# Wider norm sums, dilated attention cut into steps, six banks for two tails, and held condition sums in a four-layer block stack

## The chip, the core and the metric

The kernel runs on one core of one Trainium2 chip. The metric is the device time of one execution in microseconds (us). In the texts PE is TensorE (matrix products; its clock is granted at one of two levels, 2.4 or 1.2 GHz), PEld its weight loads, DVE is VectorE, ACT is ScalarE, POOL is GpSimd and SP is SyncE, which issues the transfers from memory.

## The reference, cut to what matters

Four residual layers stand one behind the other, each on 256 tokens of 1024 values. The first two (the first block) end each half with a layer norm; the second two (the second block) begin each part with an rms norm. The parts that the change touches:

```python
def layer_norm(x, g, b):
    xf = x.astype(jnp.float32)
    xc = xf - jnp.mean(xf, -1, keepdims=True)
    var = jnp.mean(xc * xc, -1, keepdims=True)
    return (xc * lax.rsqrt(var + LN_EPS) * g.astype(jnp.float32) + b.astype(jnp.float32)).astype(x.dtype)
...
    # first block, layer i: mixer (retention, then neighbourhood attention), feed-forward
        m_lat = jnp.split(cond_lat @ ada_w[i] + ada_b[i], 6, axis=-1)
        h_lat = layer_norm(DEEPNORM_ALPHA * h_lat + m_lat[2] * y_lat, ln_g[i, 0], ln_b[i, 0])
        f_lat = swiglu(modulate(h_lat, m_lat[3], m_lat[4]), ffn_w13[i], ffn_w2[i])
        h_lat = layer_norm(DEEPNORM_ALPHA * h_lat + m_lat[5] * f_lat, ln_g[i, 1], ln_b[i, 1])
...
    # second block, layer l: feed-forward, hybrid mixer, feed-forward
        u = modulate_2(rmsnorm(h, ln_mix[l]), sh2, sc2)
        m = hybrid_mixer(u, w_in[l], conv_w[l], a_log[l], dt_bias[l], dn_norm[l], w_a[l], w_b[l], w_o[l])
        h = h + gt2[:, None, :] * m
...
    # in hybrid_mixer: a gated delta rule of 8 heads, and dilated attention of 12 heads of 64
    for window, dilation in DA_PATTERNS:
        o_p, lse_p = dilated_window_branch(qd, kd, vd, slopes, window, dilation)
    ...
    y_b = o_b.reshape(B, S, DA_WIDTH) @ w_b
    merged = jax.nn.sigmoid(gate_a) * y_a + jax.nn.sigmoid(gate_b) * y_b
    return merged @ w_o
```

Layer 0 carries a second stream of 256 tokens (the context) through both halves.

## The kernel before

All tokens lie along the columns: h is [128, 8, 256], eight blocks of 128 features by 256 tokens. Every weight product is made three times (high by high, high by low, low by high), with both operands split into a high part fp32r and the rest. Weights are streamed: SP loads a chunk of 128x1024 into w_raw, ACT makes w_hi, DVE makes w_lo, a few chunks ahead of use. One product row is 256 or 512 tokens wide and takes its weights from the chunk.

The order of all instructions is written by the program itself and kept on the chip (a manual schedule): each engine executes its own instructions in the order in which they are emitted. While the products are emitted, other work (generators called sides) is pumped in between. class Times (line 29) keeps planned times: busy is a clock for each engine, when() gives the time at which a tile is planned to be written or read. A side yields WAIT when its next step isn't due by PE's planned clock; with force set it emits regardless.

- Norm (line 692): squares by ACT, then sums over the features by PE. sums (line 767) takes the tile as stationary operand and a tile ones [128, 1] as the moving one, so that each sum is one column. In fp32 one such product is two records in the trace. stats (line 782) reads the sums, makes mean and scale, and spread copies them over 128 rows by four transposes (ident,n_st).
- PSUM has eight banks: four acc, two mm, two tr. bank(many) (line 304) takes a bank of mm, or with many=True the earlier of mm and acc. outp(3), the last retention output products (line 1269), and the last part of Layer0's feed-forward (line 1381 on) run with many=False, so on the two mm banks.
- ada_gen (line 434) makes the condition vectors on DVE: the products of a weight tile are added into ada_acc, a transpose and a reduction make ada_part, and reduce_one (line 486) folds it by one PE product into a tr bank.
- The hybrid (class at line 1660, its run at 1697): projections into q, k, v of the delta rule, z, and the dilated q, k, v; the chains of the delta rule and the convolutions are sides. dilated (line 2093) treats six pairs of heads ("a head" below is one n, its two 64-row halves i = 0 and 1). first makes the scores of both halves in two tr banks, adds the distances (DVE), takes two maxima per half (DVE) and two exponentials per half (ACT). normalize multiplies and sums (DVE), and scales (ACT). second(0) and second(1) transpose (PE) and copy (ACT) one half each; third multiplies with the values (PE) and splits the result (ACT ah, DVE al). pipeline (line 255) emits the stage that is due, the last stage first.
- gate_b: the products of the second gate come in four pairs; their evacuation writes into sb, where the dilated values lie, so the second pair first calls finish on the dilated side:

```python
        def gate_b(i):
            if i:
                da.finish()
            p = (i + 3) % 4
            return sb[:, 2 * p:2 * p + 2, :]
...
    def finish(self):
        while not self.done:
            self.b.forced(self.step)
```

## Time and profile before

| | |
|---|---|
| median of 3 runs | 2873.59 us (2870.81 to 2875.27) |
| profiled execution | 2875.96 us |
| its span | 2874.1 us |
| mean granted clock of PE | 0.977 |
| busy: PE, PEld | 2776.9 us (97%), 2548.0 us (89%) |
| busy: DVE, ACT, POOL | 2097.7 us (73%), 1322.0 us (46%), 290.0 us (10%) |

The profiled execution's time is its span and 1.9 us around it. Busy time of PE counts an instruction until its modelled end, so PE's rows overlap; the distance of two starts is what one costs. The granted clock is a share of 2.4 GHz: 0.50 is 1.2 GHz. A stretch of the trace is read by the engines' busy times in it and its granted clock; the timeline gives each row's start, its length and, in brackets, the idle time ahead of it with the instruction that ended it.

### The profile page before, as it was taken

The numbers are of one execution on the slowest core, as the hardware profiler recorded it, in microseconds if no ns is written. First come the engines' busy times: TensorE is split into PE (matmuls) and PEld (weight loads), VectorE is DVE, ScalarE is ACT, GpSimd is POOL, SyncE is SP. The second block draws the span as 40 slices with busy tenths as digits, with TensorE's granted clock in tenths as the row PEclk, the third lists the DMA queues.
The fourth block names the chain that finished last, engine by engine and source line by source line (L and its number), as shares of the span: only waits on it lengthen the run. The fifth ranks groups of instructions, "written<-read, shape, count | busy, mean of one in ns | idle before, by whom it ended". The sixth has DMA issues, their size and how long they took to land.

```text
span 2874.1 us, 49237 instructions
## 1 busy us (share of the span) xinstructions
PE 2776.9 (97%) x19349; PEld 2548.0 (89%) x19349; DVE 2097.7 (73%) x3396; ACT 1322.0 (46%) x2318; POOL 290.0 (10%) x363
## 2 busy tenths in 40 slices
PE   8999998999998998998999989999999999999999
PEld 4878887888877778998999989999999998899999
DVE  5888886887877776787877777788565577676754
ACT  4433323422224544444445665554454456655543
POOL 0000002000002100001002123210010022130100
PEclk9999998999998998998999999999999999999999
DMA  7444441576755543775886533458566654324564
GB/s 232 155 129 144 141 154 63 190 234 211 239 180 144 122 149 117 253 255 157 267 261 199 155 92 115 147 173 273 186 181 184 186 172 118 89 82 153 179 183 133
DMA packets 433245, 488.34 MB, mean 170 GB/s; under 512 B 34651, under 2 KB 362301, under 8 KB 433013
## 3 DMA queue, kind: packets, MB, share of 16 engines
q1 hardware_dynamic: 431972, 484.59, 54.1%
q8 instruction: 152, 2.49, 0.4%
q10 hardware_dynamic: 1040, 0.60, 0.1%
q14 instruction: 81, 0.66, 0.1%
HBM read 484.07 MB, written 1.05 MB: 169 GB/s over the span
## 4 chain that ended last, share of the span: by engine, by line
PE 82%; DVE 8%; ACT 4%; issue 3%; DMA 1%; SPq 1%; POOL 1%; ACTq 0%; DVEq 0%; POOLq 0%
PE ps_acc L75 46%; PE ps_mm L75 32%; PE ps_tr L75 4%; DVE w_lo L75 2%; ACT w_hi L75 2%; DVE n_t L75 1%; DMA ada_w<-ada_w 1%; ACT n_a L75 1%; DVE n_a L75 1%; DVE h L75 1%; DVE al L75 1%; SPq L75 1%; DVE ada_acc L75 0%; DVE da_st L75 0%; ACT ah L75 0%
## 5 line engine op out<-in xcount | busy, mean ns | idle before, releaser
L75 DVE TENSOR_TENSOR w_lo<-w_raw,w_hi 128x1024 fp32r<-128x1024 f32 (+1 forms) x672 | 816.5, 1226 | 426.5 <-ACT w_hi L75 420.8
L75 ACT ACTIVATE w_hi<-w_raw 128x1024 fp32r<-128x1024 f32 (+2 forms) x686 | 699.7, 1032 | 490.3 <-PE ps_acc L75 233.9
L75 PE MATMUL ps_mm<-ah,w_hi 128*128 128x256 f32 (+1 forms) x2288 | 707.0, 309 | 8.1 <-DVE q_lo L75 3.0
L75 PE MATMUL ps_mm<-ah,w_lo 128*128 128x256 f32 (+1 forms) x2288 | 680.8, 298 | 4.0 <-POOL w_lo L75 2.3
L75 PE MATMUL ps_mm<-al,w_hi 128*128 128x256 f32 (+1 forms) x2288 | 681.7, 298 | 0.2
L75 PEld LDWEIGHTS ps_mm<-ah,w_hi 128*128 128x128 f32 x2288 | 434.9, 190 | 31.4 <-issue 11.1
L75 PEld LDWEIGHTS ps_mm<-ah,w_lo 128*128 128x128 f32 x2288 | 435.2, 190 | 18.9 <-POOL w_lo L75 3.4
L75 PEld LDWEIGHTS ps_mm<-al,w_hi 128*128 128x128 f32 x2288 | 435.7, 190 | 12.4 <-DVE al L75 1.0
L75 PE MATMUL ps_acc<-ah,w_hi 128*128 128x256 f32 (+2 forms) x1440 | 436.4, 303 | 2.3 <-ACT w_hi L75 2.3
L75 PE MATMUL ps_acc<-ah,w_lo 128*128 128x256 f32 (+2 forms) x1440 | 433.5, 301 | 1.4 <-DVE w_lo L75 1.3
L75 PE MATMUL ps_acc<-al,w_hi 128*128 128x256 f32 (+2 forms) x1440 | 433.3, 301 | 0.0
L75 DVE SCALAR_TENSOR_TENSOR ada_acc<-ada_w,cact,ada_acc 128x512 f32<-128x512 f32 x476 | 354.4, 759 | 16.8 <-DMA ada_w<-ada_w 11.8
L75 PEld LDWEIGHTS ps_acc<-ah,w_lo 128*128 128x128 f32 x1440 | 274.7, 191 | 12.5 <-DVE w_lo L75 2.6
L75 PEld LDWEIGHTS ps_acc<-ah,w_hi 128*128 128x128 f32 x1440 | 274.5, 191 | 12.2 <-ACT w_hi L75 2.5
L75 PEld LDWEIGHTS ps_acc<-al,w_hi 128*128 128x128 f32 x1440 | 274.8, 191 | 9.6
L75 PE MATMUL ps_acc<-hh,w_hi 128*128 128x256 f32 (+1 forms) x866 | 255.5, 295 | 0.0
L75 PE MATMUL ps_acc<-hh,w_lo 128*128 128x256 f32 (+1 forms) x866 | 255.2, 295 | 0.0
L75 PE MATMUL ps_acc<-hl,w_hi 128*128 128x256 f32 (+1 forms) x866 | 254.9, 294 | 0.0
L75 POOL TENSOR_TENSOR n_a<-n_a 128x512 f32<-128x512 f32 (+1 forms) x28 | 40.4, 1444 | 1292.6 <-ACT n_a L75 1292.1
L75 PEld LDWEIGHTS ps_acc<-hh,w_hi 128*128 128x128 f32 x866 | 163.2, 188 | 4.4
L75 PEld LDWEIGHTS ps_acc<-hl,w_hi 128*128 128x128 f32 x866 | 163.2, 188 | 4.4
L75 PEld LDWEIGHTS ps_acc<-hh,w_lo 128*128 128x128 f32 x866 | 163.0, 188 | 4.4
(391 smaller groups left out, 4368.5 us busy)
## 6 DMA issues: line engine op xcount, KB each, us to landing
ada_w<-ada_w SPq DMA_DIRECT2D x448, 256.0 KB
w_raw<-w_in SPq DMA_DIRECT2D x132, 512.0 KB
w_raw<-ffn_w SPq DMA_DIRECT2D x128, 512.0 KB
w_raw<-ffn_wg SPq DMA_DIRECT2D x88, 512.0 KB
w_raw<-ffn_wu SPq DMA_DIRECT2D x88, 512.0 KB
w_raw<-ffn_wd SPq DMA_DIRECT2D x80, 512.0 KB
w_raw<-ret_w_in SPq DMA_DIRECT2D x48, 512.0 KB
w_raw<-na_w_qkv SPq DMA_DIRECT2D x24, 512.0 KB
```

Of the source, the lines that this page charges most:

```text
L75: r = f(*args, **kw)
```

## The change

Five edits:

1. The sums use avg (128x128, each value 1/256) as the moving operand in place of ones; each sum becomes 128 equal columns, of which stats reads the first and multiplies by 256/D.
2. outp(3) and the last down part run with many=True.
3. The dilated attention has eight stages in place of five: first, soft(0), soft(1), normalize(0), normalize(1), second(0), second(1), third. The first five have a spare of 1.0: they are due only when DVE's planned busy time is at most 1.0 us ahead of PE's planned clock. The limits name the same stages by their new numbers.
4. In ada_gen a fold waits until the part is planned to be written.
5. warm(16): sixteen products of two constant tiles into an mm bank, between the last layer norm of the first block and the first rms norm.

```diff
-        self.ones = cp.tile([128, 1], F32, name="ones")
-        nc.vector.memset(self.ones, 1.0)
...
-                            if not self.force and self.free("ps_tr", self.BANKS["tr"]) > self.clock:
+                            when = max(self.free("ps_tr", self.BANKS["tr"]),
+                                       self.times.when(self.times.written, self.pending[0][2]))
+                            if not self.force and when > self.clock:
                                 yield WAIT
...
+    def warm(self, n):
+
+        ps = self.ps("mm")
+        for _ in range(n):
+            self.nc.tensor.matmul(ps[:, :128], self.ident, self.avg, start=True, stop=True)
...
-                    nc.tensor.matmul(self.p[i][:, o:o + 1], x[:, 128 * t:128 * t + 128], b.ones,
+                    nc.tensor.matmul(self.p[i][:, 128 * o:128 * o + 128], x[:, 128 * t:128 * t + 128], b.avg,
...
-        p, st = self.p[i], self.s[i][1]["st"]
+        p, st = self.p[i].rearrange("p (a n) -> p a n", n=128)[:, :, 0], self.s[i][1]["st"]
...
-            ts(st[:, 0:4], p[:, 0:4], 1.0 / D, None, op0=OP.mult)
+            ts(st[:, 0:4], p[:, 0:4], 256.0 / D, None, op0=OP.mult)
...
-            return b.gemm_b(self.o[h], lambda k: (yh[:, k, :], yl[:, k, :]), 512, self.residual(gates, norms), ks=4, many=norms is None)
+            return b.gemm_b(self.o[h], lambda k: (yh[:, k, :], yl[:, k, :]), 512, self.residual(gates, norms), ks=4, many=True)
...
-                           self.residual(gates, self.norms if part == NP - 1 else None), ks=2 * (f1 - f0), many=part < NP - 1))
+                           self.residual(gates, self.norms if part == NP - 1 else None), ks=2 * (f1 - f0), many=True))
...
-                st = P.tile([128, 2, 4], F32, name="da_st", bufs=4)
+                S[n].append((s, P.tile([128, 2, 4], F32, name="da_st", bufs=4)))
+
+        def soft(i):
+            def f(n):
+                s, st = S[n][i]
                 for t, (a, z) in enumerate(segs):
                     nc.vector.tensor_reduce(st[:, t, 0:1], s[:, a:z], axis=AX.X, op=OP.max, negate=True)
                 for t, (a, z) in enumerate(segs):
                     nc.scalar.activation(s[:, a:z], s[:, a:z], AF.Exp, bias=st[:, t, 0:1])
-                S[n].append((s, st))
-
-        def normalize(n):
-            for s, st in S[n]:
+            return f
+
+        def normalize(i):
+            def f(n):
+                s, st = S[n][i]
...
-        stages = ((first, lambda: "tr2", (3, lambda: 2)), (normalize, None, None), (second(0), tr, (4, lambda: 1)), (second(1), tr, None),
-                  (third, tr, None))
+        stages = ((first, lambda: "tr2", (6, lambda: 2), 1.0), (soft(0), None, None, 1.0), (soft(1), None, None, 1.0),
+                  (normalize(0), None, None, 1.0), (normalize(1), None, None, 1.0), (second(0), tr, (7, lambda: 1)),
+                  (second(1), tr, None), (third, tr, None))
...
         n.finish()
+        b.warm(16)
         n2 = Norm(b, "rms", slow=False)
```

How the order of the instructions moves, at three places. First PE in Layer1's norm, between the neighbourhood attention's output products (o_hi, o_lo with w_hi, w_lo): before,

```order
L75 MATMUL ps_acc<-o_hi,w_lo 128x256
L75 MATMUL ps_tr<-ones,n_a 128x1 x2
L75 MATMUL ps_tr<-ones,h 128x1 x2
L75 MATMUL ps_tr<-ones,n_a 128x1 x2
L75 MATMUL ps_tr<-ones,h 128x1 x2
```

and after:

```order
L75 MATMUL ps_acc<-o_hi,w_lo 128x256
L75 MATMUL ps_tr<-avg,n_a 128x128 x2
L75 MATMUL ps_tr<-avg,h 128x128 x2
L75 MATMUL ps_tr<-avg,n_a 128x128 x2
L75 MATMUL ps_tr<-avg,h 128x128 x2
```

Nothing moves there; the sums have 128 columns instead of one.

Second, DVE in the first hybrid at the second and the first dilated head (n_a<-da_dist is a score row, da_st<-n_a its maxima, da_mult the normalization; d_ tiles belong to the chains, n_t and cv_x to the convolutions, ada_ to the condition vectors): before,

```order
L75 TENSOR_TENSOR w_lo<-w_raw,w_hi 128x1024
L75 SCALAR_TENSOR_TENSOR n_a<-da_dist,ps_tr 128x384
L75 TENSOR_REDUCE da_st<-n_a 128x1 x2
L75 SCALAR_TENSOR_TENSOR n_a<-da_dist,ps_tr 128x384
L75 TENSOR_REDUCE da_st<-n_a 128x1 x2
L75 SCALAR_TENSOR_TENSOR n_a,da_st<-n_a,da_mult 128x128
L75 SCALAR_TENSOR_TENSOR n_a,da_st<-n_a,da_mult 128x256
L75 RECIPROCAL da_st<-da_st 128x2
```

and after:

```order
L75 TENSOR_TENSOR d_XX<-d_XX,ps_acc 128x256
L75 SCALAR_TENSOR_TENSOR ada_acc<-ada_w,cact,ada_acc 128x512
L75 SCALAR_TENSOR_TENSOR n_a<-da_dist,ps_tr 128x384 x2
L75 TENSOR_TENSOR w_lo<-w_raw,w_hi 128x1024
L75 SCALAR_TENSOR_TENSOR n_t<-cv_x,cwT,n_t 128x255
L75 SCALAR_TENSOR_TENSOR n_t<-cv_x,cwT,n_t 128x254
L75 SCALAR_TENSOR_TENSOR n_t<-cv_x,cwT,n_t 128x253
```

The maxima and the normalization no longer follow the scores; weight splits, convolutions and condition rows come between, and the first head begins later.

Third, PE in the first hybrid at the products of gate_b (ps_mm<-ah or al with w_hi or w_lo; ident,n_a are the transposes of second, da_k,da_q the scores of first, n_t,sb and da_pt,sb the products of third): before, at one of the last two heads of the dilated attention, among the products,

```order
L75 MATMUL ps_mm<-ah,w_lo 128x256
L75 MATMUL ps_acc<-ident,d_XX 128x128 x2
L75 MATMUL ps_acc<-d_XX,d_t_15494 128x128 x2
L75 MATMUL ps_tr<-ident,n_a 128x128 x3
L75 MATMUL ps_mm<-ah,w_hi 128x256
```

and after, behind the last product of the second gate_b pair:

```order
L75 MATMUL ps_mm<-ah,w_lo 128x256
L75 MATMUL ps_tr<-ident,n_a 128x128 x6
L75 MATMUL ps_tr<-da_k,da_q 128x128 x2
L75 MATMUL ps_tr<-da_k,da_q 128x256 x2
L75 MATMUL ps_tr<-n_t,sb 64x128
L75 MATMUL ps_tr<-da_pt,sb 64x128
```

After these rows 27 more of the same four kinds follow before the next weight product: four times the six transposes in all, two times the scores, four times the six products of third, with nothing else on PE between. The second hybrid has a piece of the same form behind its second gate_b pair.

## Rows read from the trace of the kernel before

**Rows 1.** The page: its first line, and the chain by engine.

```profile
span 2874.1 us, 49237 instructions
...
PE 82%; DVE 8%; ACT 4%; issue 3%; DMA 1%; SPq 1%; POOL 1%; ACTq 0%; DVEq 0%; POOLq 0%
```

**Rows 2.** Stretches by engine (columns in the first line), the two norms of the first block.

```profile
core 0: us, PE busy (x) PEld busy (x) DVE busy (x) ACT busy (x) POOL busy (x), PEclk, DMA share, GB/s
1094.00:1097.70 3.70, 2.47 (x21) 2.24 (x20) 2.40 (x5) 2.64 (x7) 0.00 (x0) 1.00 0.40 134
1097.80:1114.80 17.00, 17.00 (x81) 17.00 (x81) 9.18 (x16) 5.15 (x9) 0.00 (x0) 0.50 0.20 63
1316.20:1336.70 20.50, 14.18 (x64) 13.52 (x64) 11.76 (x27) 10.85 (x24) 0.70 (x1) 0.50 0.18 58
```

**Rows 3.** Timeline of PE (start, length, instruction, count): Layer1's norm.

```profile
1098.78 0.99 PE L75 MATMUL ps_tr<-ones,h 128*128 128x1 f32 x4
...
1115.37 0.58 PE L75 MATMUL ps_tr<-ones,n_a 128*128 128x1 f32 x4
...
1119.23 0.60 PE L75 MATMUL ps_tr<-ident,n_st 128*128 128x128 f32 x4
```

**Rows 4.** Timeline of DVE, same stretch; the brackets hold the idle time before, and its end.

```profile
1105.99 0.88 DVE L75 SCALAR_TENSOR_TENSOR h<-ps_acc,v_lat,h 128x256 f32<-128x256 f32 x2 [1.95 <-PE ps_acc L75]
...
1116.44 0.16 DVE L75 TENSOR_SCALAR n_st<-ps_tr 128x4 f32<-128x4 f32 x1 [5.18 <-PE ps_tr L75]
```

**Rows 5.** Timeline of PE: Layer0's first norm, the first block's last norm, the end.

```profile
471.76 0.47 PE L75 MATMUL ps_mm<-v_hi,w_hi 128*128 128x512 f32 x1 [3.66 <-DVE h L75]
...
486.65 1.12 PE L75 MATMUL ps_tr<-ident,n_st 128*128 128x128 f32 x4 [1.43 <-POOL n_st L75]
...
1325.52 1.87 PE L75 MATMUL ps_tr<-ones,n_a 128*128 128x1 f32 x8 [3.95 <-ACT n_a L75]
...
2865.37 4.02 PE L2232 MATMUL ps_acc<-ident,h 128*128 128x128 f32 x16 [0.51 <-DVE h L2226]
```

**Rows 6.** Timeline of PE, first hybrid: the longest wait.

```profile
1675.81 1.22 PE L75 MATMUL ps_acc<-d_XX,d_t 128*128 128x128 f32 x4 [4.84 <-DVE d_MQ L75]
```

**Rows 7.** Stretches by engine: the half-clock piece, and 80 us of each hybrid.

```profile
1674.60:1681.40 6.80, 5.59 (x26) 5.59 (x27) 4.73 (x18) 3.55 (x9) 0.73 (x1) 0.50 0.45 126
1660.00:1740.00 80.00, 71.52 (x587) 66.71 (x587) 57.36 (x153) 48.80 (x126) 14.19 (x22) 0.96 0.32 96
2428.00:2508.00 80.00, 71.42 (x589) 66.57 (x588) 53.83 (x146) 49.44 (x129) 14.76 (x23) 0.96 0.27 80
```

**Rows 8.** Timeline of DVE: half a head (scores, maxima), then normalization of two halves.

```profile
1711.37 0.56 DVE L75 SCALAR_TENSOR_TENSOR n_a<-da_dist,ps_tr 128x384 f32<-128x384 f32 x1
...
1713.59 0.28 DVE L75 SCALAR_TENSOR_TENSOR n_a<-n_a,da_mult 128x128 f32<-128x128 f32 x1
...
1714.35 0.64 DVE L75 SCALAR_TENSOR_TENSOR n_a<-n_a,da_mult 128x128 f32<-128x128 f32 x1
```

**Rows 9.** Timeline of ACT: exponentials or scalings of two halves, copies, a gate.

```profile
1671.28 1.54 ACT L75 ACTIVATE n_a<-n_a,da_st 128x128 f32<-128x128 f32 x4 [0.82 <-DVE da_st L75]
...
1697.34 0.49 ACT L75 ACTIVATE n_t<-ps_tr 128x384 f32<-128x384 f32 x1
...
1737.52 0.39 ACT L75 ACTIVATE ah<-ps_tr 128x256 fp32r<-128x256 f32 x1 [0.43 <-PE ps_tr L75]
...
1767.27 0.60 ACT L75 ACTIVATE sb<-ps_mm 128x512 f32<-128x512 f32 x1
```

**Rows 10.** Timeline of PE: scores of one head, transposes, first and last product with values.

```profile
1664.76 1.29 PE L75 MATMUL ps_tr<-da_k,da_q 64*128 64x128 f32 x8
...
1695.89 0.32 PE L75 MATMUL ps_tr<-n_t,sb 128*64 128x128 f32 x1
...
1696.50 0.27 PE L75 MATMUL ps_tr<-da_pt,sb 128*64 128x128 f32 x1
...
1700.06 0.49 PE L75 MATMUL ps_tr<-ident,n_a 128*128 128x128 f32 x3
```

More of the change, by code (lines that the diff above doesn't have):

```diff
@@ L791, in stats @@
         else:
-            ts(st[:, 0:2], p[:, 0:2], 1.0 / D, EPS, op0=OP.mult, op1=OP.add)
+            ts(st[:, 0:2], p[:, 0:2], 256.0 / D, EPS, op0=OP.mult, op1=OP.add)
         nc.gpsimd.tensor_tensor(out=st[:, 0:2], in0=st[:, 0:2], in1=b.mhalf[:, 0:2], op=OP.pow)
@@ L2129, in normalize @@
                     nc.scalar.activation(s[:, a:z], s[:, a:z], AF.Copy, scale=st[:, t, 2:3])
+            return f
         def second(i):
```

## The prediction

> **What bounds the kernel now.** I read the page's chain first: TensorE (PE) holds 82% of it, VectorE (DVE) 8%, ScalarE (ACT) 4% [rows 1]. So a microsecond counts only where PE stands still or runs at 1.2 GHz instead of 2.4. I then asked for stretches with their granted clock, and for PE's timeline where the stretch was slow. Two kinds of places came out that the change touches. The first kind is the norms. In Layer1's norm PE was busy 17.00 of 17.00 us, and yet the granted clock was 0.50, the 1.2 GHz level [rows 2]. What PE did before the fall was one-column sums, back to back. The same sums take 0.99 us for four records at the half clock and 0.58 at the full one, and four 128-column transposes take 0.60 at the full one, as much as four one-column records [rows 3]. So PE's time is the same for 1 and for 128 columns; what can differ is the clock that is granted after them. The second kind is the hybrids. There PE waits 4.84 us for DVE's d_MQ [rows 6], since DVE first does two heads' scores and a whole normalization; the half clock of the next 6.8 us follows from that wait [rows 7].
>
> **The sums with 128 columns, and the warm matmuls.** They remove and add no PE time by themselves; the gain is the clock. I take each place by what ends last there.
> - Layer1's norm: at the full clock 17.0 us of PE work would be 8.5, the most there is. DVE waits 1.95 and 5.18 us for PE in it, 7.1 together [rows 4]; beyond that DVE and ACT bound. The last spread at 1119.23 [rows 3] would come near 1113. I take 6, from 4.5 to 7.1.
> - Layer0's first norm, with the six banks for the last retention products: PE waits 3.66 us for DVE's h, because the two mm banks are full. Six banks let PE go on, but DVE still has the same h to add, so a part only moves. With it the tail speeds up: eight sums by 0.41 (0.99 less 0.58) per four records at the half clock, the four transposes of the spread from 1.12 to 0.60 [rows 3, 5]. I take 3, from 0 to 5.5. Layer0's second norm has the same form with its last part down: 2.5, from 0 to 5.5.
> - The first block's last norm: 20.5 us at the half clock, PE busy 14.18 [rows 2]. Half of that, 7.1, is the ceiling, but in its middle PE waits for ACT's n_a, 3.95 us first [rows 5]. Only the ends count: I take 3, from 1 to 5. The 16 warm matmuls are 32 records; eight take 1.87 us at the half clock [rows 5], so they need about 7 us there and 3.5 at the full one. At the full clock they fit in the 3.95 us wait and cost nothing; at the half clock 3 us would stick out. That end is in the range.
> - The end: sixteen transposes take 4.02 us [rows 5], and at the full clock about 2; ACT's copies behind them take part of that. I take 1.5, from 0 to 2.
> Sum of the norms: 16, from 6 to 25.
>
> The Trainium skill, page "TensorE: Matmul & The Clock Gate", Part 1, "What's actually happening", says that the gate follows how busy PE has been recently. Rows 2 speak against it as it stands: PE was busy all the time and had 1.2 GHz. By that rule the wider sums would bring nothing, and of the 16 only the banks' part would stay.
>
> **The condition sums held.** The fold of a finished condition sum waits until DVE is planned to have written it. Up to the second norm the order of the instructions is unchanged but for the shapes and banks, so the waits there stay. Later it moves a fold of a quarter us here and there. I take 0, from -2 to 2.
>
> **The dilated attention in steps: what it removes.** In 80 us of each hybrid PE is busy 71.52 and 71.42, so it stands still 8.5 and 8.6 us; and in the 6.8 us at half clock half of 5.59 us of work is lost, 2.8 in the first and by the same form about 2.4 in the second [rows 7]. Together 22. The new order has half as much of DVE's dilated work in one piece: two scores, then a weight split, and the maxima rows later (the order of DVE above). But with these gaps DVE gets convolution and condition rows; a wait of 1 to 2 us remains in places. I take 19, from 10 to 22. What is late next is the step that waits for ACT's copy of a chain, some tenths each.
>
> **What it adds.** The five first stages start only when DVE's planned backlog is at most 1 us. They are so put off that when the second gate_b pair's evacuation calls da.finish(), more than three of six heads are still open. finish() forces them, and PE's order shows it: 24 transposes, two heads' scores and four products with values stand in one piece with no weight product between (the order of PE above). Before, the last head's copy was at 1737.52 and this evacuation at 1767.27, so nothing was forced [rows 9]. PE executes in order, so the later products wait, though their weights are there. The same happens in both hybrids.
>
> Price, first hybrid. ACT has 13 pairs of exponentials or scalings at 0.77 (1.54 for two), 8 copies at 0.49 and 4 at 0.39 [rows 9]: 15.5 us. DVE has 6 pairs of maxima, two heads' scores, 7 normalizations and 4 subtractions: scores with maxima are 1.11 per half (1711.37 to 1713.59 for two), a normalization 0.76 [rows 8], a subtraction about ACT's 0.39: 12.4. PE has 8 transposes of three, two scores and four products with values, from 0.88 (1695.89 to 1696.77), 1.29 and 0.49 [rows 10], less the overlap of neighbours: 7.5. If ACT alone bound, the piece lasts 15.5; if nothing overlaps, 35. Followed through the order row by row (a score needs both ps_tr banks, so it waits for the copies of the head before; a product with values needs both halves' copies; each row begins when its engine and what it reads are free), it comes to 23. PE's 7.5 stood among products before, so PE loses 15.5, from 8 to 27. The second hybrid has 11 pairs, 6 copies and 4 heads' ends: ACT 13, all 31; followed through, 22, of which PE works 7: loss 15, from 6 to 24.
>
> To this comes the clock. One wait of 4.84 us brought 6.8 us at 1.2 GHz, most of it after PE had work again [rows 6, 7]. A piece in which PE works a third of the time will run mostly at 1.2: I add 3 us inside each and 2.5 after each, 11 together, from 0 to 13. Added in both: 15.5 + 15 + 11 = 41, from 14 to 64; I believe 32 to 46.
>
> **The sum.** 2875.96 (the profiled execution) - 16 (norms) - 19 (waits removed) + 41 (forced pieces) = 2882. The runs' median, 2873.59, lies 2.4 under the profiled one, so I say 2880, 6 us or 0.2% slower. About 0.2% is what a measurement of this kernel can tell from no change.
>
> **Rivals.**
> 1. The forced pieces are nearly hidden: DVE and ACT come to them with a lead, PE enters late, and the clock holds. The mechanism is in gate_b(1): if the open heads' maxima and scalings are done before PE gets there, only ACT's bound is left, 8 + 6 = 14 for both. Then 2874 - 16 - 19 + 14 = 2853. It decides from the point where the pieces together cost less than 35 (16 + 19); from 29 down it is faster by over 0.2%. For it: ACT is busy only some 60% of these 80 us [rows 7]. Against it: the last weight product and the first forced row have nothing but a few chain rows between them.
> 2. The wide sums don't hold the clock (the rule of the skill's page, worked out by rows): of the norms' 16 only the banks' 3 stay, so 2880 + 13 = 2893. For it: PE was fully busy and the clock fell all the same; what it counts, these rows don't say. Against it: the 128-column transposes at 1119.23 run at 0.60 for four, the full clock [rows 3], and the hybrids are full of such rows at a granted clock of 0.96 in the mean [rows 7].
> 3. The steps don't remove the waits: condition rows on DVE take the place of the dilated ones, so the 22 us stay with new names. Removed 5 rather than 19: 2894. For it: the new order has condition rows among the steps in the first hybrid (the order of DVE above). Against it: the second hybrid has none left.
> 4. The change doesn't do what it says, in the norms' timeline: the three or four places at half clock are off the chain, gain under 6 and the pieces as said: 2890. It is counted with rival 2.
>
> **Chances.** Forecast 0.50 (slower 0.30, within 0.2% 0.20, since it lies at that edge); rival 1 0.25 (faster 0.22, same 0.03); rival 2 with 4 0.13 (slower 0.11, same 0.02); rival 3 0.12 (slower 0.08, same 0.04). So faster 0.22, same 0.29, slower 0.49. The forecast's own range is 2868 to 2890. The range of 8 in 10 leaves out the best of rival 1 and the worst of 2 and 3: 2855 to 2898.
>
> **What would show it.** Right: in both hybrids, just before the second tanh of sb, PE's timeline shows waits for ACT's n_a, n_t and da_pt of 10 to 18 us in sum over 20 to 27 us, at 0.50 over part of it; and the 4.84 us wait for d_MQ is gone. In Layer1's norm the granted clock is 1.00 and its 17 us are about 11. Wrong: waits there under 7 us in each hybrid (rival 1), 0.50 in Layer1's norm (rival 2), or idle time above 6 us per hybrid ahead of the forced piece (rival 3).

## The result, and the profile after

The changed kernel takes 2888.34 us (median of 4 runs, 2887.55 to 2890.55), the kernel before 2874.24 beside it: a ratio of 1.0052, 95% interval 1.0035 to 1.007. It is slower by 14 us, where 6 us were forecast; the time lies in the range. The profiled execution took 2890.55 us.

The page after, its first lines and the chain [rows 1]:

```profile
span 2888.8 us, 49302 instructions
## 1 busy us (share of the span) xinstructions
PE 2775.7 (96%) x19381; PEld 2534.4 (88%) x19381; DVE 2097.6 (73%) x3395; ACT 1324.0 (46%) x2318; POOL 293.3 (10%) x363
...
PE 77%; DVE 11%; ACT 6%; issue 3%; DMA 2%; POOL 0%; SPq 0%; ACTq 0%; DVEq 0%; POOLq 0%
```

Laid beside each other at the same instructions, the two traces say where the 14 us come from. At the first norm's spread the changed kernel is 2.0 us ahead; at Layer0's second norm 5.2 more; at Layer1's norm 6.8 more; from there, over the first block's last norm, to the start of the first hybrid 4.5 more, 18.5 us in all. The first hybrid then loses 19.4 us and the second 15.7; the feed-forwards behind them and the end give back 2.0. Sum: -18.5 + 35.1 - 2.0 = 14.6 us, but for rounding the difference of the spans (2888.8 to 2874.1). The first of these numbers is good to some us only: the traces of kernels of this study whose instructions are the same up to the first hybrid reach it between 1508.4 and 1514.9 us.

Stretches of the changed kernel, by engine, with the granted clock: Layer1's norm (two rows), the half-clock pieces in the first and second hybrid, and the 196 us ahead of each of these pieces.

```profile
core 0: us, PE busy (x) PEld busy (x) DVE busy (x) ACT busy (x) POOL busy (x), PEclk, DMA share, GB/s
1084.00:1100.00 16.00, 13.59 (x96) 12.82 (x96) 11.61 (x24) 7.88 (x15) 0.00 (x0) 0.89 0.27 83
1100.00:1109.00 9.00, 9.00 (x79) 9.00 (x78) 4.24 (x9) 1.64 (x4) 0.70 (x1) 1.00 0.19 58
1767.80:1791.70 23.90, 19.53 (x92) 12.99 (x93) 9.87 (x40) 12.46 (x32) 0.74 (x1) 0.50 0.00 0
2535.80:2556.30 20.50, 14.38 (x64) 8.72 (x65) 8.19 (x40) 11.47 (x31) 0.00 (x0) 0.50 0.00 1
1566.00:1762.00 196.00, 180.41 (x1474) 172.67 (x1475) 149.02 (x327) 118.66 (x315) 58.74 (x82) 0.98 0.41 122
2333.00:2529.00 196.00, 186.57 (x1538) 180.51 (x1538) 139.44 (x300) 119.25 (x296) 50.30 (x76) 0.98 0.39 117
```

In Layer1's norm the 17 us at 0.50 [rows 2] are gone: the clock is 0.89 and then 1.00. In the hybrids two new stretches of 23.9 and 20.5 us stand at 0.50. There PE executes the forced piece. Its timeline in the first hybrid, cut to the longest waits, the scores and the end:

```profile
1762.07 0.49 PE L75 MATMUL ps_tr<-ident,n_a 128*128 128x128 f32 x3
1765.17 0.84 PE L75 MATMUL ps_tr<-ident,n_a 128*128 128x128 f32 x3 [2.60 <-ACT n_a L75]
1766.63 0.48 PE L75 MATMUL ps_tr<-da_k,da_q 64*128 64x128 f32 x2 [0.63 <-ACT n_t L75]
1767.70 1.60 PE L75 MATMUL ps_tr<-da_k,da_q 64*128 64x128 f32 x6 [0.58 <-ACT da_pt L75]
...
1773.38 2.35 PE L75 MATMUL ps_tr<-da_k,da_q 64*128 64x128 f32 x8
...
1780.46 1.09 PE L75 MATMUL ps_tr<-ident,n_a 128*128 128x128 f32 x3 [1.75 <-ACT n_a L75]
...
1789.01 1.22 PE L75 MATMUL ps_acc<-d_XX,d_MT 128*128 128x128 f32 x4
```

From 1762.07 to 1789.01 there is no weight product. The waits in brackets are those that the prediction named, for ACT's n_a, n_t and da_pt and shortly for DVE. Together they come to 8.1 us here and 7.6 in the second hybrid. The clock falls behind the first three of them, at 1767.8, and stays at 0.50 until 1791.7, just after the weight products are back; most of the rest of the loss is the clock's, by an estimate below.

Ahead of the piece the waits were to vanish. The waits of the changed kernel's PE from 1566 to 1762, longest first (engine, tile waited with, what ended it: us in total, times, longest):

```profile
PE ps_acc L75 <- ACT d_vb L75: 3.1, 1, 3.1
PE ps_acc L75 <- DVE d_XX L75: 2.9, 2, 2.3
PE ps_acc L75 <- ACT d_t L75: 2.6, 4, 1.2
```

The 4.84 us wait for d_MQ [rows 6] is gone, but the whole list sums to 15.9 us, where that of the kernel before over 196 us at the same distance from its hybrid's start (1584 to 1780) sums to 11.4. In the second hybrid, over the 176 us from 2354 to 2530 in both, it is 8.3 after 10.5. In the first hybrid nothing was saved, in the second 2.2 us.

### The profile page after: what moved, and what is told of

It reads as the page before. It is cut to its first block, busy times and chain, and to the rows that moved or that the text cites. A ratio compares the mean times of both kernels' runs of the same rounds, so it can differ in the third digit from the quotient of the medians.

```text
span 2888.8 us, 49302 instructions
## 1 busy us (share of the span) xinstructions
PE 2775.7 (96%) x19381; PEld 2534.4 (88%) x19381; DVE 2097.6 (73%) x3395; ACT 1324.0 (46%) x2318; POOL 293.3 (10%) x363
## 4 chain that ended last, share of the span: by engine, by line
PE 77%; DVE 11%; ACT 6%; issue 3%; DMA 2%; POOL 0%; SPq 0%; ACTq 0%; DVEq 0%; POOLq 0%
PE ps_acc L75 44%; PE ps_mm L75 28%; PE ps_tr L75 4%; DVE w_lo L75 3%; ACT w_hi L75 2%; DVE n_t L75 1%; DMA ada_w<-ada_w 1%; ACT n_a L75 1%; DVE h L75 1%; DVE n_a L75 1%; DVE ada_acc L75 1%; DVE al L75 1%; ACT n_t L75 1%; DVE d_XX L75 1%; ACT ah L75 0%
## 5 line engine op out<-in xcount | busy, mean ns | idle before, releaser
L75 DVE SCALAR_TENSOR_TENSOR ada_acc<-ada_w,cact,ada_acc 128x512 f32<-128x512 f32 x476 | 353.2, 756 | 15.2 <-DMA ada_w<-ada_w 10.2
L75 PEld LDWEIGHTS ps_acc<-ah,w_lo 128*128 128x128 f32 x1440 | 273.4, 190 | 12.8 <-DVE w_lo L75 3.1
L75 PEld LDWEIGHTS ps_acc<-ah,w_hi 128*128 128x128 f32 x1440 | 272.8, 189 | 12.8 <-ACT w_hi L75 3.1
L75 PE MATMUL ps_acc<-hh,w_hi 128*128 128x256 f32 (+1 forms) x890 | 265.0, 298 | 0.0
L75 PE MATMUL ps_acc<-hl,w_hi 128*128 128x256 f32 (+1 forms) x890 | 264.2, 297 | 0.0
L75 PE MATMUL ps_acc<-hh,w_lo 128*128 128x256 f32 (+1 forms) x890 | 264.2, 297 | 0.0
```

What stands on the lines that cost most here:

```text
L75: r = f(*args, **kw)
```

## The experiments

All times stand beside runs of the kernel before on the same chip (2874.5 to 2875.2 us in the three sets). The table has one line for each kernel whose hybrids matter. "us" is the median of the runs; the other columns come from the one profiled execution of each kernel. A hybrid counts from the spread of its norm to that of the next norm. The five kernels with the old attention and the old rate of condition rows (two of the table, three of the norms' part below) have 384.9 to 386.8 us in the first and 377.9 to 379.4 in the second, so a difference of hybrids below 2 us says nothing. "waits" is the sum of PE's list of waits in it (its entries are rounded, so a sum is good to 0.4), "half" the us at a granted clock of 0.50 in both, "ACT for da_st" the idle time of ACT in the first hybrid ahead of attention instructions that wait for DVE's da_st.

| kernel | us | first hybrid | second | waits, first + second | half | ACT for da_st |
|---|---|---|---|---|---|---|
| before | 2874.2 | 386.8 | 377.9 | 19.4 + 14.1 | 17.0 | 14.5 |
| changed | 2888.3 | 406.2 | 393.6 | 28.0 + 20.0 | 58.0 | 10.9 |
| old attention | 2851.9 | 385.2 | 379.2 | 18.3 + 14.0 | 17.0 | 14.5 |
| steps, no spare | 2858.9 | 391.7 | 379.1 | 22.7 + 15.2 | 13.6 | 35.6 |
| steps, spare 2 | 2869.9 | 403.8 | 377.9 | 27.1 + 11.4 | 23.9 | 27.7 |
| split by engine, halves | 2872.2 | 396.4 | 387.2 | 22.3 + 18.6 | 30.7 | 0 |
| split by engine, heads | 2853.4 | 387.2 | 377.0 | 19.9 + 13.8 | 10.2 | 0.9 |
| the same, few condition rows | 2843.7 | 378.5 | 377.1 | 12.8 + 13.7 | 13.6 | 0 |
| old attention, few condition rows | 2848.1 | 379.0 | 377.9 | 14.8 + 14.3 | 13.6 | 14.9 |
| old attention, no softmax | 2851.0 | 385.8 | 375.6 | 18.5 + 11.4 | 17.0 | 0 |

Changed against old attention: the hybrids are 35.4 us longer. The waits are 15.7 us longer. Of the 41.0 us more at the half clock PE works 32.2 (in the rest it waits, which is counted already), and half of that, 16.1, is taken as lost: eight score records take 2.35 us at 0.50 in the timeline above and 1.29 at the full clock [rows 10], not quite twice as long. By this estimate the two make 31.8 of the 35.4 us.

### The change without its attention, and the attention without the rest

The first kernel is the changed one with the five old stages; the second is the kernel before with the eight new ones. The edit that both turn on (undone in the first, done alone in the second):

```
-        stages = ((first, lambda: "tr2", (3, lambda: 2)), (normalize, None, None), (second(0), tr, (4, lambda: 1)), (second(1), tr, None),
-                  (third, tr, None))
+        stages = ((first, lambda: "tr2", (6, lambda: 2), 1.0), (soft(0), None, None, 1.0), (soft(1), None, None, 1.0),
+                  (normalize(0), None, None, 1.0), (normalize(1), None, None, 1.0), (second(0), tr, (7, lambda: 1)),
+                  (second(1), tr, None), (third, tr, None))
```

> The changed kernel with the old dilated attention (five stages, no spare): norms, six banks, warm-up and held condition sums are as in the change. Theory: between the two traces the norms and their surroundings gained 19.5 us, and the two hybrids lost 19.4 and 15.7 us, all of the loss by the dilated steps. The time is then 2888.3 - 35 = 2853 us (2850 to 2857), faster than both kernels. Rival, the loss in the hybrids comes from the condition sums being held (their rows move in the hybrids too): the time stays at 2880 or more, and the 20 us pieces stay at full size. Rival, the gain of the norms is bound to the rest: 2870 or more.

> The kernel before with the dilated steps alone (eight stages, spare 1.0), nothing else of the change. Theory: the steps alone cost what the hybrids lost, 35 us, on the old norms: 2874.2 + 35 = 2909 us (2904 to 2914), and the pieces without weight products stand ahead of the second tanh of each hybrid's gate projection as in the changed kernel. Rival, the condition sums are needed for the loss: 2874 to 2885.

Measured: 2851.86 us (5 runs, ratio 0.9928, 0.9915 to 0.9940) and 2910.90 us (4 runs, ratio 1.0127, 1.0111 to 1.0142). The attention costs 36.5 us on the new norms (2888.3 less 2851.9) and 36.2 on the old ones (2910.9 less 2874.7). So it is the attention alone, and its cost doesn't hang on the rest. What is left of the change gains 22.8 us.

### The spare

From here on a diff is against the changed kernel. The first kernel:

```
-        stages = ((first, lambda: "tr2", (6, lambda: 2), 1.0), (soft(0), None, None, 1.0), (soft(1), None, None, 1.0),
-                  (normalize(0), None, None, 1.0), (normalize(1), None, None, 1.0), (second(0), tr, (7, lambda: 1)),
+        stages = ((first, lambda: "tr2", (6, lambda: 2)), (soft(0), None, None), (soft(1), None, None),
+                  (normalize(0), None, None), (normalize(1), None, None), (second(0), tr, (7, lambda: 1)),
```

The second has 2.0 in place of each 1.0.

> The changed kernel with the eight stages of the dilated attention, but without the spare of 1.0 us, so that a step no longer waits for VectorE's planned backlog to be under 1 us; everything else as in the change. By the order of instructions no piece of more than a few dilated rows without weight products is left. Theory (the spare makes the forced piece, and the steps by themselves save little, 1.5 us net over both hybrids): 2853 us (2848 to 2858), the same as with the old dilated attention. Prediction's term (the steps take away 19 us of waits, the forced pieces alone cost): 2853 - 19 = 2834 us, with 4 to 9 us fewer idle us in each hybrid. Rival (the steps themselves cost, by their finer grain, not the spare): 2880 or more.

> The changed kernel with a spare of 2.0 us instead of 1.0 us in the dilated steps. By the order of instructions one short piece of 6 dilated rows stands together in the first hybrid, against 16 in each hybrid at 1.0. Theory (the cost is the forced piece's length): 2853 to 2860 us. Rival (a spare of any size holds the attention back to the end of the gate projection and costs by that): 2870 or more. Prediction's term (a spaced-out attention without the forced piece keeps the waits away): 2834 to 2840.

Measured: 2858.91 us without the spare (ratio 0.9950, 0.9937 to 0.9962), 2869.90 with 2.0 (11 runs, 0.9984, 0.9975 to 0.9993). The forced piece is the spare's: without it 29.4 of the 36.5 us go. But the steps save nothing: without the spare they are 7.0 us slower than the old stages, just above my range, and the prediction's 2834 is 25 us off. A spare of 2.0 is 11 us slower than none, all of it in the first hybrid and most of it ahead of the place where the changed kernel has its piece; my expectation by the length of the piece missed. In the second hybrid that kernel's PE waits 11.4 us, 2.6 less than with the old stages, so steps can take a little away; the hybrid is as long as in the kernel before, 377.9.

Where the steps lose without the spare is seen on three engines in the first hybrid. That kernel's timeline of PE (start, length, instruction, count, the wait before it):

```profile
1712.32 0.38 PE L75 MATMUL ps_acc<-ident,d_XX 128*128 128x128 f32 x2
1715.85 0.49 PE L75 MATMUL ps_acc<-ident,d_MT 128*128 128x128 f32 x2 [3.15 <-ACT d_t L75]
```

Its timeline of ACT, whose copy d_t PE waits for:

```profile
1712.84 1.49 ACT L75 ACTIVATE n_a<-n_a,da_st 128x128 f32<-128x128 f32 x4 [2.65 <-DVE da_st L75]
1714.24 1.04 ACT L75 ACTIVATE w_hi<-w_raw 128x1024 fp32r<-128x1024 f32 x1
...
1715.34 0.36 ACT L75 ACTIVATE d_t<-ps_acc 128x256 f32<-128x256 f32 x1
```

Its timeline of DVE, for whose da_st ACT waits:

```profile
1711.65 0.95 DVE L75 SCALAR_TENSOR_TENSOR n_a<-n_a,da_mult 128x256 f32<-128x256 f32 x1
...
1712.64 0.17 DVE L75 RECIPROCAL da_st<-da_st 128x2 f32<-128x2 f32 x1
```

A step issues its ACT half right behind its DVE half. ACT comes to it early, stands idle for 2.65 us until DVE's reciprocal, and the weight split and the delta rule's copies queue behind it. In the whole first hybrid ACT's idle time of this kind is 35.6 us, and PE waits 17.1 us for ACT, where it is 14.5 and 4.7 with the old stages (the 15.1 and 3.2 of the next expectation are of a shorter stretch).

### The steps' halves apart

To take that wait away, each step was cut by engine: peak is the maxima (DVE), expo the exponentials (ACT), total the weighted sums (DVE), scale the scalings (ACT), with the same instructions as before. An ACT stage is issued when the planner takes the DVE stage as done. The first kernel does it for each half of a head (below), the second for both halves at once.

```
+        stages = ((first, lambda: "tr2", (10, lambda: 2)), (peak(0), None, None), (peak(1), None, None),
+                  (expo(0), None, None), (expo(1), None, None), (total(0), None, None), (total(1), None, None),
+                  (scale(0), None, None), (scale(1), None, None), (second(0), tr, (11, lambda: 1)),
+                  (second(1), tr, None), (third, tr, None))
```

> The changed kernel with each attention step split once more, by engine, and no spare: the two maxima (VectorE), the two exponentials (ScalarE), the two weighted sums (VectorE) and the two scalings (ScalarE) of a pair of heads are eight stages of their own, and a ScalarE stage is issued only when the planner takes its VectorE stage as done; all else as in the change. In the trace of the steps without spare ScalarE stood idle 35.6 us in the first hybrid ahead of attention instructions that waited for da_st of VectorE (14.5 us with the old stages), and TensorE's waits for ScalarE rose from 3.2 to 15.1 us. Theory (ScalarE's half of a step stands in its queue behind an unfinished VectorE half, with the delta rule's copies behind it): that idle time falls under 10 us, TensorE's waits for ScalarE to 3 to 6 us, and the time is at or below that of the old stages, 2840 to 2852 us. Rival (the steps cost by their grain, whatever their order on ScalarE): 2858 us or more. Prediction's term (steps can take away up to 19 us of waits, once ScalarE isn't blocked): 2833 us.

> As the kernel before this one in the list, but each of the four stages takes both heads of a pair at once (maxima, exponentials, sums, scalings: four stages). Theory (the order by engine counts, not the grain): ScalarE's idle time ahead of da_st under 10 us in the first hybrid and 2840 to 2852 us. Rival (the grain counts: whole pairs are what made the old stages better than the steps): faster than the half-wise split by 5 us or more. Rival (neither: what moves the time is the exact place of the chain's links): above 2852 us though the idle time falls.

Measured: 2872.24 us (11 runs, 0.9992, 0.9983 to 1.0001) and 2853.40 (5 runs, 0.9928, 0.9914 to 0.9941). The idle time did go: the first kernel's list of ACT's waits has no row of da_st, and this is the second kernel's in the first hybrid (us in total, times, longest):

```profile
ACT n_a L75 <- DVE da_st L75: 0.9, 1, 0.9
```

PE's waits did not: 40.9 us in the two hybrids by halves, 33.7 by heads, 32.3 with the old stages. Against the steps without the spare, 37.9, the split by halves takes the same halves of a head and has no such idle time, and PE waits no less. So the blocked queue decides what PE waits for, not how long, and that theory falls as the cause of the cost. By halves it is 18.8 us slower than by heads, with the same order of engines; the rival by grain (how much one step takes) said so, the theory's 2840 to 2852 was missed by both, and the third rival (above 2852 though the idle time falls) fits too. But the number of stages isn't all that differs. By halves the attention again ends late, and a piece stands on PE without weight products in each hybrid, 10.8 and 7.5 us long, with a granted clock below 1 in both; by heads no dilated piece is longer than 2.0 us. The two pieces by halves (columns as in the stretches above):

```profile
1752.00:1762.80 10.80, 8.71 (x51) 6.34 (x50) 5.09 (x12) 7.01 (x19) 0.00 (x0) 0.73 0.38 116
2528.00:2535.50 7.50, 5.90 (x45) 4.79 (x44) 4.22 (x9) 3.49 (x9) 0.11 (x1) 0.77 0.35 107
```

How much of the 18.8 us is the grain and how much these pieces was not separated.

### Is the attention what PE waits for at all?

The softmax is taken out of the kernel with the old attention, on DVE and ACT (the diff is against that kernel):

```
-                slope = float(np.float32(2.0) ** np.float32(-8.0 * (2 * n + i + 1) / 12))
+                slope = 0.0
...
-                st = P.tile([128, 2, 4], F32, name="da_st", bufs=4)
-                for t, (a, z) in enumerate(segs):
-                    nc.vector.tensor_reduce(st[:, t, 0:1], s[:, a:z], axis=AX.X, op=OP.max, negate=True)
-                for t, (a, z) in enumerate(segs):
-                    nc.scalar.activation(s[:, a:z], s[:, a:z], AF.Exp, bias=st[:, t, 0:1])
-                S[n].append((s, st))
+                S[n].append((s, None))
...
         def normalize(n):
-            for s, st in S[n]:
...
+            pass
```

> The changed kernel with the old five stages of the dilated attention, and the softmax left out of it: no maxima, exponentials, weighted sums and scalings (VectorE and ScalarE), and a slope of 0; TensorE's work is the same. With the old stages TensorE waits 18.3 us in the first hybrid and 14.0 in the second. Prediction's term (19 us of the waits come from the attention's rows on VectorE and ScalarE, and go when these give way): both together fall under 16 us and the time to 2830 to 2840 us. Theory now (the waits are the delta rule's own links and the weight splits beside them; the attention only decides where they show): they stay at 24 us or more, and the time at 2845 to 2853 us.

Measured: 2851.00 us (4 runs, 0.9918, 0.9904 to 0.9931), against 2851.86 with the softmax. The second hybrid shows it best, since it has no condition rows. There DVE's busy time falls by 16.5 us and ACT's by 14.8, and no condition rows take their place. PE's longest waits in it with the old attention; the whole list sums to 14.0:

```profile
PE ps_acc L75 <- DVE d_MQ L75: 4.8, 1, 4.8
PE ps_acc L75 <- DVE d_XX L75: 3.9, 4, 1.9
```

The same list of the kernel without softmax, sum 11.4:

```profile
PE ps_acc L75 <- ACT d_XX L75: 3.1, 2, 2.9
PE ps_acc L75 <- DVE d_XX L75: 2.5, 2, 1.6
```

The wait for d_MQ, ahead of which the prediction saw the attention, goes, and a wait for ACT's d_XX comes. With the rows gone PE waits 2.6 us less in the second hybrid, which is 3.6 us shorter (2.3 against the kernel before). In the first, where condition rows moved into the gap (54 of them for 41), it waits 18.5 for 18.3, and by the medians the whole kernel is 0.9 us faster. "Theory now" held, in waits and in time. That another order of the rows can hardly give more than to take them out is argued, not shown; 19 was predicted.

### The condition rows

```
-            b.ada.rate = 0.2 if step == 1 else 1.2
+            b.ada.rate = 0.02 if step == 1 else 1.2
```

> The four stages by engine (maxima, exponentials, sums, scalings of a pair of heads), and the condition rows held back in the hybrids: their rate 0.02 in place of 0.2, so that 6 of them stand among the first hybrid's delta rule on VectorE in place of 29 (the second has none in either). Rival 3 of the prediction (condition rows take the place of the attention's): TensorE's waits in the first hybrid fall from 19.9 us to 10 or less, the time from 2853.4 to 2840 to 2845 us. Theory now (the second hybrid has no condition rows and still 13.8 us of waits, so they are not the cause): 2849 to 2855 us.

> The old five stages of the dilated attention, everything else of the change, and the same low rate of the condition rows in the hybrids (5 rows in place of 26 in the first hybrid). Rival 3: TensorE's waits in the first hybrid fall from 18.3 us to 10 or less, 2851.9 to 2842 or less. Theory now: 2848 to 2854 us.

Measured: 2843.73 us (4 runs, 0.9892, 0.9879 to 0.9906) and 2848.11 (4 runs, 0.9906, 0.9892 to 0.9921). In the first "theory now" missed and rival 3 had the time, though not the waits (12.8, not 10); the second lies at the edge of "theory now". A stretch that counts only DVE's rows which write or read ada_acc, the accumulator of the condition sums (us, DVE's busy time and rows, granted clock, DMA): the first hybrid of the kernel split by heads:

```profile
1509.80:1897.00 387.20, 30.78 (x41) 0.99 0.47 145
```

The same with the low rate:

```profile
1509.50:1888.00 378.50, 4.42 (x6) 0.99 0.43 127
```

26 us of DVE's work leave the first hybrid and it is 8.7 us shorter, its waits 7.1; with the old stages 6.2 and 3.5. By the medians the low rate is worth 9.7 us with the split by heads and 3.7 with the old stages. The second hybrid, where nothing changed, keeps its 13.7 and 14.3. The stretch between the hybrids, which takes the rows, is 0.5 us longer. Split by heads with few condition rows is the fastest kernel of this study, 31 us below the one before and 45 below the changed one.

### The parts of the norms

All three have the old attention beside the edit shown. One column (stats then reads the columns as in the kernel before):

```
-                    nc.tensor.matmul(self.p[i][:, 128 * o:128 * o + 128], x[:, 128 * t:128 * t + 128], b.avg,
+                    nc.tensor.matmul(self.p[i][:, o:o + 1], x[:, 128 * t:128 * t + 128], b.ones,
```

> The changed kernel with the old dilated attention and, beside it, the old sums of the norms: one column (a vector of ones) in place of 128. What is left of the change: banks, warm-up, held condition sums. Theory (the 128 columns gave the gains at Layer0's second norm, 5.3 us, at Layer1's norm, 6.8, at the end, 1.2, and some of the last norm's): 2851.9 + 10 to 14 = 2862 to 2866 us, with Layer1's norm again at a granted clock of 0.50 and 17 us. Rival (the gain there is the banks' or the warm-up's): 2852 to 2856 us.

Two banks and no warm-up:

```
-            return b.gemm_b(self.o[h], lambda k: (yh[:, k, :], yl[:, k, :]), 512, self.residual(gates, norms), ks=4, many=True)
+            return b.gemm_b(self.o[h], lambda k: (yh[:, k, :], yl[:, k, :]), 512, self.residual(gates, norms), ks=4, many=norms is None)
...
-                           self.residual(gates, self.norms if part == NP - 1 else None), ks=2 * (f1 - f0), many=True))
+                           self.residual(gates, self.norms if part == NP - 1 else None), ks=2 * (f1 - f0), many=part < NP - 1))
...
-        b.warm(16)
```

> The changed kernel with the old dilated attention and without the six banks (both places) and the 16 warm-up products: what is left is the 128 columns and the held condition sums. Theory (columns give 13 to 15 of the norms' 22.8 us, as their absence cost 15.2): the banks' part is 2 to 4 us, at Layer0's two norms, the warm-up's 2 to 4 us, at the last norm of the first block: 2856 to 2860 us. Rival (the columns alone hold the clock, so that banks and warm-up bring nothing): 2851 to 2854 us. Rival (the columns only work with them): 2865 or more.

Condition sums not held:

```
-                            when = max(self.free("ps_tr", self.BANKS["tr"]),
-                                       self.times.when(self.times.written, self.pending[0][2]))
-                            if not self.force and when > self.clock:
+                            if not self.force and self.free("ps_tr", self.BANKS["tr"]) > self.clock:
```

> The changed kernel with the old dilated attention and with condition sums that are not held for their last addition. Theory (the predicted 0 for this part): 2850 to 2854 us, the same as with them held, 2851.9. Rival (the held sums keep TensorE from waiting for a sum that isn't there): 2855 or more. Rival (holding moves rows into the hybrids and costs there): 2849 or less.

Measured, beside the 2851.86 us of the kernel with everything but the steps: one column 2867.08 (8 runs, 0.9976, 0.9965 to 0.9986), so the columns are worth 15.2; without banks and warm-up 2856.73 (5 runs, 0.9938, 0.9925 to 0.9952), so these two are worth 4.9 together; sums not held 2853.03 (5 runs, 0.9923, 0.9910 to 0.9935), no difference that can be told.

The one-column kernel spreads over 7 us and its profiled execution is its fastest, while that of the kernel with 128 columns is its slowest, so the two traces show only 8 of the 15 us. Its stretches around Layer0's first and second norm, Layer1's norm and the first block's last (columns as in the stretches above):

```profile
462.00:488.00 26.00, 22.58 (x103) 20.06 (x102) 18.14 (x33) 6.71 (x11) 13.24 (x9) 0.74 0.14 41
856.00:882.00 26.00, 22.53 (x109) 19.90 (x108) 21.07 (x36) 6.31 (x9) 10.28 (x7) 0.78 0.39 122
1084.00:1110.00 26.00, 24.09 (x175) 23.21 (x174) 16.52 (x36) 9.17 (x18) 0.70 (x1) 0.87 0.30 101
1304.00:1330.00 26.00, 22.18 (x153) 21.73 (x153) 15.42 (x37) 12.12 (x27) 1.39 (x2) 0.80 0.32 104
```

The same stretches of the kernel with 128 columns and the old attention:

```profile
461.00:487.00 26.00, 20.63 (x111) 17.27 (x110) 19.54 (x34) 7.51 (x12) 13.25 (x9) 0.95 0.13 41
855.00:881.00 26.00, 19.90 (x119) 16.94 (x117) 21.72 (x37) 6.35 (x10) 10.29 (x7) 1.00 0.39 122
1082.00:1108.00 26.00, 22.64 (x173) 21.67 (x172) 16.21 (x34) 9.51 (x19) 0.70 (x1) 0.93 0.27 88
1298.00:1324.00 26.00, 20.93 (x172) 19.86 (x171) 17.52 (x39) 11.91 (x27) 1.40 (x2) 1.00 0.39 130
```

At each norm PE is busier with one column and has the lower clock. In Layer1's norm it isn't the 0.50 and 17 us that I expected, from the kernel before, whose same 26 us read:

```profile
1096.00:1122.00 26.00, 25.08 (x148) 25.08 (x149) 12.76 (x27) 7.64 (x15) 0.70 (x1) 0.67 0.13 41
```

The timeline of PE there, with one column:

```profile
1092.68 0.58 PE L75 MATMUL ps_tr<-ones,h 128*128 128x1 f32 x4
...
1095.36 0.77 PE L75 MATMUL ps_tr<-ones,h 128*128 128x1 f32 x4
```

This time the sums begin at the full clock, 0.58 us for four, and it falls only at the eighth group, for a shorter time. Why it held longer here is open.

What the warm-up does is seen in the kernel without it. The timeline of PE at the first block's last norm:

```profile
1307.16 0.65 PE L75 MATMUL ps_tr<-ident,n_st 128*128 128x128 f32 x4 [1.49 <-POOL n_st L75]
1311.75 2.08 PE L75 MATMUL ps_tr<-avg,n_a 128*128 128x128 f32 x8 [3.94 <-ACT n_a L75]
```

After a wait of 3.94 us eight records take 2.08. The same place in the changed kernel, where the warm-up's 32 records take the place of that wait and the sums take about half:

```profile
1306.70 5.36 PE L75 MATMUL ps_mm<-avg,ident 128*128 128x128 f32 x32
1311.90 1.06 PE L75 MATMUL ps_tr<-avg,n_a 128*128 128x128 f32 x8
```

The warm-up is longer than the wait, and the first sum comes 5.7 us behind the spread's start (1306.22) where it comes 4.6 behind it without. From the last layer norm's spread to the rms norm's it is 16.8 to 18.4 us in the traces with 128 columns and the warm-up, 17.45 in the one with 128 columns alone and 20.3 in the kernel before. So what was gained at this place is the columns' for the most part, and a gain of the warm-up's own is not shown; the banks and the warm-up were not taken out one by one.

## Why the prediction was right in direction and where it failed

**Waits removed by the steps, -19: failed.** This is the step that was wrong. In the trace DVE did the attention's rows just ahead of d_MQ, and I took the rows as the cause of PE's idle time. Measured, the hybrids lost 35.1 us and the forced pieces explain 32.6 by the estimate below, so the steps removed nothing and added 2.5; by the runs, without the spare, they add 7.0. The kernel without softmax bounds the term: with the rows gone altogether PE waits 2.6 us less in the second hybrid. The trace of before already had a sign of it. Inside the 4.84 us wait [rows 6] DVE ends its attention rows at 1672.0 and then stands idle itself, by its timeline:

```profile
1673.80 1.23 DVE L75 TENSOR_TENSOR w_lo<-w_raw,w_hi 128x1024 fp32r<-128x1024 f32 x1 [1.81 <-ACT w_hi L75]
```

ACT's w_hi (1672.72) stands behind four of the attention's rows, and d_MQ (1675.27) behind this weight split. So several engines stood in that wait, and I priced only one. Ahead of the pieces most of PE's waits are for tiles of the delta rule, before and after. That the links of its chain, where one engine hands over to the next, set the idle time, and that whoever stands ahead of a link only gets the name, is argued: no run changed the delta rule. What sets the 14 us in the second hybrid is open; the softmax's rows account for 2.6 of it, and condition rows, of which it has none, for nothing.

**Forced pieces, +41: right, by two errors.** Both pieces came where the order showed them. I had 30.5 us for idle time and 11 for the clock. Measured are 15.6 of waits (8.05 and 7.59), and 19.53 and 14.38 us of PE's work at the half clock, of which half is taken as lost, 17.0: together 32.6, an estimate beside the 29.4 us by which the kernel without the spare is faster. That the sum came near is luck: the waits were put too high and the clock too low. The sign that I named, waits of 10 to 18 us in each piece, did not come. Followed through the order row by row the piece was to last 23 us with 7.5 of PE's work; it lasts 26.9, but PE's rows at 1.2 GHz fill much of the time in which I saw it wait.

**Norms, -16: right, a little low.** By the two traces: Layer0's first norm 2.0 (3 predicted), its second 5.2 (2.5), Layer1's 6.8 (6), the last 4.5 (3), the end 0.8 (1.5); 19.3 in all, and 22.8 by the runs with the old attention. The clock in Layer1's norm rose as said, to 0.89 and 1.00. Of DVE's two waits for PE there, 7.1 us together [rows 4], the first is gone and the second is 1.64, by these rows of DVE's timeline after:

```profile
1095.67 0.87 DVE L75 SCALAR_TENSOR_TENSOR h<-ps_acc,v_lat,h 128x256 f32<-128x256 f32 x2
...
1102.58 0.16 DVE L75 TENSOR_SCALAR n_st<-ps_tr 128x4 f32<-128x4 f32 x1 [1.64 <-PE ps_tr L75]
```

That the warm-up fits in the 3.95 us wait was wrong: its 32 records take 5.36 us.

What is late next in Layer0's second norm is POOL, by PE's timeline after:

```profile
878.62 0.65 PE L75 MATMUL ps_tr<-ident,n_st 128*128 128x128 f32 x4 [2.80 <-POOL n_st L75]
```

**Condition sums held, 0: right**, 2853.03 without and 2851.86 with.

**The sum.** 2880 forecast; the norms gained 3.3 more, the pieces cost 8.4 less, and where 19 were to go 2.5 were added: -3.3 - 8.4 + 21.5 = +9.8, against 8 measured. The feed-forwards, which the sum leaves out, gave back 1.2. The direction came out since the pieces and the missing gain outweigh the norms.

**The rivals.** Rival 1 (pieces nearly hidden, 14 us, and a clock that holds) was half right: the waits came out at 15.6, near its 14 and far from my 30.5, but the clock did not hold. Its sign, under 7 us in each hybrid, was missed by little. Rival 2 and the Trainium skill's rule behind it ("TensorE: Matmul & The Clock Gate", Part 1, "What's actually happening": the gate follows how busy PE has been) would have kept the norms at 0.50. This case's stretches speak against busy time alone: PE is busy 19.53 of 23.90 us in the forced piece at 0.50, and 20.93 of 26.00 at the last norm with 128 columns at 1.00, nearly the same share. Rival 3 had the outcome, waits that stay, and put it at 2894 with the pieces. Its cause is a part of the truth: DVE's rows on ada_acc in the first hybrid went from 33 to 40 with the steps, and a low rate of condition rows is worth 3.7 us with the old stages and 9.7 with those split by heads; the second hybrid has none. It was not tried on the changed kernel itself. Its signal, more than 6 us of idle time ahead of the piece, was there in both (15.6 and 9.4, from the stretches' 196 us). But the kernel before has 11.4 us of waits in 196 us of the first hybrid and 10.5 in 176 of the second: the signal should have been a difference. I gave this rival 0.12; it should have had more, because the trace of before named the neighbour of a wait, and that is no test of the cause.

## What to carry to other kernels

The instruction that stands ahead of a late one isn't yet its cause: before a gain is put on moving it, take it out altogether, which shows about how much there is to gain (here 2.6 us in a hybrid, where some 9 were expected). A condition that holds work back needs a look at the place where that work is forced: put off by a spare of 1 us, it came due in one piece without weight products, and the clock made the piece about twice as dear as its waits. Sums that take PE as long with 128 columns as with one were worth 15 us here when made wide.

## What was not expected of the hardware

By the estimate above the clock cost more than the waits in a stretch where PE was busy most of the time: from 1767.8 to 1791.7 PE was busy 82% at 0.50, on transposes and products with 64 rows or columns, after waits of 2.60, 0.63 and 0.58 us. And one-column sums don't always lose the clock: over 26 us of Layer1's norm the one-column kernel has 0.87 in the mean, the kernel before 0.67, with 17 us of them at 0.50 [rows 2]; no run here shows what made the difference.
